# Expert stage of a hybrid attention and mixture-of-experts layer: a third tile form with two half experts in plain fp32, and the shared expert's rows kept on chip

## The chip, the cores and the metric

One NeuronCore of a Trainium2 chip runs the whole layer as one program. The metric is the device time of an execution in microseconds (us); before the change it is 1123.37 us, the median of three runs.

## The reference

The layer is a hybrid attention block, a layer norm, a mixture of experts and a second layer norm, on 512 tokens of width 1024, in fp32. Only the mixture of experts matters here. Each token picks 8 of 64 experts; an expert is two matrices 1024x256 (w1, w3) and one 256x1024 (w2), 3 MB of weights in all, and a shared expert of the same shape sees every token:

```
scores = sigmoid(hf @ w_router)                 # 512 x 64, then top 4 of 8 groups, top 8 experts
hb = silu(x_e @ w1_e[e]) * (x_e @ w3_e[e])      # x_e: the tokens of expert e
acc[t] += (hb @ w2_e[e]) * w[:, None]           # w = weight of the token for e, scaled by 2.5
shared = (silu(hf @ ws1) * (hf @ ws3)) @ ws2
out = layer_norm(ALPHA * h + acc + shared, ln2_g, ln2_b)
```

The routing of the given inputs, counted from the reference, sends 37 to 105 tokens to an expert (mean 64).

## The kernel before

The first 400 us (projections, two attentions) are not touched. The expert stage follows. `order()` ranks the 60 dynamic experts by their number of tokens and lays them in a list `q` = 4..63 (experts 0 to 3 are static, and come first). Work goes by **tiles** of 128 token slots: six tiles hold one expert (four static ones and the two fullest), 29 tiles hold a pair, a fuller and an emptier one; in a pair the rows of both go through both experts, with weight 0 where a row belongs to one alone. For each tile the kernel

- builds the list of its rows (`one_hot`, `slot_mm`, `tile_list`) and gathers them from `hD` in DRAM by an indirect DMA on GpSimd's queue, the **gather** (L1193), two tiles ahead;
- transposes them on TensorE (`xpose`, L1205) and splits them in two fp32r parts;
- for each expert runs 8 k-steps of w1 and w3 side by side (128x512) and, after the SiLU (`act_si`) and a transpose (`act_t`), 4 of w2. Weights come as three 1 MB pages (`expert_load`, L836, SyncE's queue). ScalarE casts each half page to fp32r (L196) and VectorE subtracts for the rest (L197): the **split**. Every product is then three fp32r matmuls (`mm3`, L317 to L319), so 36 for an expert;
- copies the result out of PSUM to a tile `y` (`finish`, L1233, ScalarE, two buffers) and adds its rows into `accD` in DRAM by an indirect accumulating DMA, the **scatter** (L1234, GpSimd's queue). `accD` was filled with ALPHA * h before.

The order of the instructions is written by hand: a list `steps` of (expert, part), with each expert's w2 parts set between the next one's w1/w3 parts. Each engine runs its own instructions strictly in that order. A page of the pool (16 pages) is free for the next load when the split has read it. All scatters write the same DRAM tensor, so each waits for the landing of the one before it; GpSimd's queue issues gathers and scatters in turn. The shared expert (`shared`, `shared_out`) is worked off in small pieces between the steps; each of its four row blocks is added to `accD` by a plain accumulating DMA (L1265) in the same chain.

The last tile is not scattered. The end loads `accD` in four blocks `zs` (L1500, after the last scatter has landed), adds the last tile with TensorE through a 0/1 matrix `back` (L1506, L1508), and normalizes.

Of the kernel before, what the change touches and what calls it, by code (L numbers as in the profile page):

```python
# [19 lines left out]
S, D = 512, 1024  # L20
NE = 64
N_STAT = 4
N_SOLO = 2
N_TILE = N_STAT + N_SOLO + (NE - N_STAT - N_SOLO) // 2
# [14 lines left out]
for _k, _w in (("cb", 128), ("dn", 256), ("dp", 256), ("ut", 128), ("inv", 8), ("tok", 8),  # L39
               ("ident", 128), ("iota1", 128), ("lt", 64), ("lte", 64), ("rq", 128), ("stat", 3)):  # L40
    _C[_k] = (_n, _n + _w)
    _n += _w
# [4 lines left out]
def const_pack():  # L47
# [20 lines left out]
    rq[N_STAT:N_STAT + N_SOLO] = np.arange(N_SOLO)  # L68
    npair = (64 - N_STAT - N_SOLO) // 2
    m = np.arange(npair)  # L70
    rq[N_STAT + N_SOLO::2] = N_SOLO + m
    rq[N_STAT + N_SOLO + 1::2] = N_SOLO + 2 * npair - 1 - m
    put("rq", np.where((np.arange(128) // 64)[None, :] == (np.arange(128) // 64)[:, None], np.tile(rq, 2)[None], -7.0))
    put("stat", np.stack([np.where(e >= N_STAT, 1.0, 0.0), np.where(e < N_STAT, 1000.0 + e, 0.0), e * 1.0], 1))
    inv = np.float32(500000.0) ** (-np.arange(0, 16, 2, dtype=np.float32) / np.float32(16))
# [55 lines left out]
def hybrid_layer_kernel(tc, xT, xn, pos, w_idx, w_blk, w_uk, w_uv, w_ab, w_o, w_r, w_s13, w_s2, w_e, ln, b_gate,  # L131
# [696 lines left out]

    def expert_load(q, eid=None, eng=()):

        src = w_e[q:q + 1] if eid is None else w_e[bass.ds(nc.sync.value_load(eid[0:1, bass.ds(q, 1)], min_val=0,
                                                                             max_val=NE - 1), 1)]
        r = []
        for i in range(3):
            t_ = page([2048], name="we")
            (G if i in eng else nc.sync).dma_start(t_, src[:, :, i * 2048:(i + 1) * 2048].rearrange("a p f -> p (a f)"))  # L836
            r.append(t_)
        return r
# [103 lines left out]
    pos1 = cpool.tile([128, 4, N_TILE], F32, name="pos1")  # L942
# [123 lines left out]
    def one_hot(pos_, i):  # L1066
        oh = t2([4, 128], BF16, name="oh")
        V.tensor_tensor(oh, C("iota1").unsqueeze(1).broadcast_to([128, 4, 128]),
                        pos_[:, :, i].unsqueeze(2).broadcast_to([128, 4, 128]), op=OP.is_equal)
        return oh  # L1070
# [15 lines left out]
    def slot_rows(pl):  # L1086
# [6 lines left out]
        return ii  # L1093
# [6 lines left out]
    def tile_list(oh, qs, tw_):  # L1100
        pl = slot_mm(oh, qs, tw_)
        return [slot_rows(pl), slot_weights(pl, len(qs))]

    tiles = [[q] for q in range(N_STAT + N_SOLO)]
    tiles += [[q, q + 1] for q in range(N_STAT + N_SOLO, NE, 2)]
# [7 lines left out]
    selt = cpool.tile([128, 4, N_TILE], BF16, name="selt")  # L1113

    def order():
# [47 lines left out]
        q0 = N_STAT + N_SOLO  # L1163
        V.tensor_copy(selt[:, :, :q0], selq[:, :, :q0])
        V.tensor_tensor(selt[:, :, q0:], selq[:, :, q0::2], selq[:, :, q0 + 1::2], op=OP.max)
        yield
        places(pos1, selt, N_TILE)
# [4 lines left out]
    def spill():  # L1172
        q0 = N_STAT + N_SOLO
        pc = ps_o()
        for c in range(4):
            mm(pc[0:1, 0:N_TILE], lhsT=ones_b[:, 0:1], rhs=selt[:, c], start=(c == 0), stop=(c == 3))
        nt = t2([3, N_TILE], name="nt")[0:1]
        for b in range(3):
            V.tensor_scalar(nt[:, b], pc[0:1, 0:N_TILE], 128.5 + 128.0 * b, None, op0=OP.is_gt)
        V.tensor_tensor(nt[:, 0], nt[:, 0], nt[:, 1], op=OP.add)  # L1180
        V.tensor_tensor(nt[:, 0], nt[:, 0], nt[:, 2], op=OP.add)
        V.tensor_copy(nbi[:, 0:q0], nt[:, 0, 0:q0])
        V.tensor_copy(nbi[:, q0:NE:2], nt[:, 0, q0:])
        V.tensor_copy(nbi[:, q0 + 1:NE:2], nt[:, 0, q0:])
        nm_ = t2([1], name="nmx")[0:1]
        V.tensor_reduce(nm_, nt[:, 0], axis=AX.X, op=OP.max)
        V.tensor_copy(nbi[:, NE:NE + 1], nm_)
# [10 lines left out]
    def gather(i):  # L1198
        xgs[i] = gather_rows(lists[i][0], xg2[i // 2 % (GA - 1)][:, i % 2])

    def xpose_to(xt, xg, q):
# [4 lines left out]
        split_to(xt[:, 0, 4 * q:4 * q + 4], xt[:, 1, 4 * q:4 * q + 4], pt.rearrange("p (k t) -> p k t", k=4))  # L1206

    def xpose(i, q):
        if q == 0:
            xts[i] = page_x([2, 8, 128], F32R, name="xt")  # L1210
        xpose_to(xts[i], xgs[i], q)
# [7 lines left out]
    def act_t(si):  # L1219
        pt = ps_o()  # L1220
        for f in range(2):
            T.transpose(pt[:, f * 128:(f + 1) * 128], si[:, f * 128:(f + 1) * 128], ident)
        at = t2([2, 2, 128], F32R, name="at")
        split_to(at[:, 0], at[:, 1], pt[:, :256].rearrange("p (f t) -> p f t", f=2))
        return at

    def finish(ii, py, last=False):
        y = t4([D], name="y")
        for n in range(2):
            if n and last:  # L1230
                V.tensor_copy(y[:, n * 512:(n + 1) * 512], py[n])
            else:
                A.copy(y[:, n * 512:(n + 1) * 512], py[n])  # L1233
        G.indirect_dma_start(out=accD[:, :], out_offset=bass.IndirectOffsetOnAxis(ap=ii[:, 0:1], axis=0),  # L1234
                             in_=y, in_offset=None, compute_op=OP.add, bounds_check=S - 1, oob_is_err=False)


    sh_si = {}
# [12 lines left out]
    def shared_out(c):  # L1251
# [6 lines left out]
        y = t4([D], name="ys")  # L1258
# [6 lines left out]
        G.dma_start(accD[c * 128:(c + 1) * 128], y, accum_op=OP.add)  # L1265
# [23 lines left out]
    def prefetch(q):  # L1289
        if q < NE and q not in wts:  # L1290
            wts[q] = expert_load(q, None if q < N_STAT else eid)

    WL = ((),(0,),(),(1,),(2,))
    tile_of = {q: i for i, tl in enumerate(tiles) for q in tl}
    steps = []
    TE = 0
    for q in range(NE + 1):
        if q == NE - 1 and TE:
            steps += [(q - 1, 4), (q - 1, 5)] + [(q, p_) for p_ in range(4)]
            continue  # L1300
        for p_ in range(4):
            if q < NE:
                steps.append((q, p_))
            if q > 0 and p_ in (2, 3):
                steps.append((q - 1, 2 + p_))
    pieces, lpend = {}, []
    todo = iter(steps)

    def split_next(eng=None):
        st_ = next(todo, None)  # L1310
        if st_ is None:
            return
        q, p_ = st_
        if p_ == 0 and eng is None:
            for j in range(q + AHEAD + 1):
                prefetch(j)
# [65 lines left out]
    for q in range(AHEAD):  # L1382
        prefetch(q)
# [3 lines left out]
    with tc.manual_schedule():  # L1387
        for n, (q, p_) in enumerate(steps):
            i = tile_of[q]
            first, last = q == tiles[i][0], q == tiles[i][-1]  # L1390
# [4 lines left out]
            if lpend and p_ == 3:  # L1395
                j, oh = lpend.pop()
                lists[j] = tile_list(oh, tiles[j], tw)
# [7 lines left out]
            if first and p_ == 1 + OHP and N_STAT <= j < len(tiles):  # L1405
                lpend.append((j, one_hot(pos1, j)))
# [6 lines left out]
            if p_ == 4 and q == NE - 2 and TE:  # L1413
                sis[q] = act_si(phs.pop(q), lists[i][1][:, q - tiles[i][0]:][:, 0:1])
                ats[q] = act_t(sis.pop(q))
            if p_ == 0 and q > 0 and q - 1 in phs:
                sis[q - 1] = act_si(phs.pop(q - 1), lists[tile_of[q - 1]][1][:, q - 1 - tiles[tile_of[q - 1]][0]:][:, 0:1])
            while len(pieces) <= LOOK and len(pieces) < len(steps) - n:
                split_next()
            hi, lo = pieces.pop((q, p_))  # L1420
            if p_ < 4:
                if p_ == 0:
                    phs[q] = ps_s()
                for r in range(2):
                    k = 2 * p_ + r
                    mm3(phs[q], xts[i][:, 0, k], xts[i][:, 1, k], hi[:, r], lo[:, r], k == 0, k == 7)
            else:
# [3 lines left out]
                for n_ in range(2):  # L1431
                    mm3(pys[i][n_], ats[q][:, 0, f], ats[q][:, 1, f], hi[:, n_], lo[:, n_], first and f == 0,
                        last and f == 1)
                if last and f == 1 and i < len(tiles) - 1:
                    finish(lists[i][0], pys.pop(i))
            if p_ == 1 and q - 1 in sis:
                ats[q - 1] = act_t(sis.pop(q - 1))
            if p_ == 1 and last and i + 1 < len(tiles):
                xpose(i + 1, 0)
            if p_ == 4 and q + 2 < NE and q + 1 == tiles[tile_of[q + 1]][-1]:  # L1440
                xpose(tile_of[q + 1] + 1, 1)
            if q == 0 and p_ == 2:
                xpose(1, 1)
            if q == NE - 1 and p_ == 3:
                sis[q] = act_si(phs.pop(q), lists[i][1][:, q - tiles[i][0]:][:, 0:1])
                ats[q] = act_t(sis.pop(q))
# [9 lines left out]
    def overflow():  # L1456

        q0 = N_STAT + N_SOLO
        with tc.If(nc.values_load(nbi[0:1, NE:NE + 1], min_val=0, max_val=3) > 0):
            posq = t2([4, NE], name="posq")  # L1460
            V.tensor_copy(posq[:, :, :q0], pos1[:, :, :q0])
            V.tensor_copy(posq[:, :, q0::2], pos1[:, :, q0:])
            V.tensor_copy(posq[:, :, q0 + 1::2], pos1[:, :, q0:])
            with tc.For_i(0, NE, 1) as q:
                with tc.If(nc.values_load(nbi[0:1, bass.ds(q, 1)], min_val=0, max_val=3) > 0):
# [4 lines left out]
                    for b in range(1, 4):  # L1470
# [113 lines left out]
```

## Time and profile before

| | us |
|---|---|
| median of three runs (1122.66 to 1123.41) | 1123.37 |
| profiled execution, its own time | 1120.32 |
| span of its instructions | 1118.5 |
| TensorE (PE) busy | 1080.3 (97%) |
| VectorE (DVE) busy | 899.9 (80%) |
| ScalarE (ACT) busy | 703.4 (63%) |

The profile is of one execution. Busy PE time is modelled, since matmuls overlap each other: a matmul's row shows its latency, and the distance between starts is what it costs. Times in rows are us from the start of the span. A row of a wait names the engine that waited, and what ended the wait as the profile infers it; where that was long done, it was another. For a DMA, "to landing" runs from its issue to the arrival of its semaphore.

### The profile page before, as it was taken

What the parts mean: (1) busy time and instruction counts of PE and PEld (TensorE: products, weight loads), DVE (VectorE), ACT (ScalarE), POOL (GpSimd) and SP (SyncE); (2) the same over time, 40 slices, a digit from 0 to 9 for tenths busy, and PEclk for the clock granted to TensorE, in tenths of its full rate; (3) what the DMA queues carried; (4) which work ended last, traced back from release to release, by engine and by line L of the source; (5) the groups of instructions that cost most, each with busy time, mean ns of one, the idle gap of its engine ahead of it and who ended that gap; (6) DMA issues with size and microseconds to landing.
All of it is one profiled execution on the core that took longest, in us unless ns stands there. A gap on an engine that the chain in (4) does not pass through costs nothing. (4 is left out here: it accounts for less than half of the span.)

```text
span 1118.5 us, 15941 instructions
## 1 busy us (share of the span) xinstructions
PE 1080.3 (97%) x5485; PEld 857.1 (77%) x5486; DVE 899.9 (80%) x1750; ACT 703.4 (63%) x1102; POOL 110.9 (10%) x83
## 2 busy tenths in 40 slices
PE   8999998999999999898999999999999999999995
PEld 7788987877778887476777777788878787878872
DVE  5678998665335978698878878899999999999986
ACT  6554353544542514287767767788888888888873
POOL 0000000000000000122211101221111111212010
PEclk9999999999999999999999999999999999999998
DMA  9414010203016558589999999999999999999943
GB/s 347 138 38 147 5 38 1 76 1 124 28 58 225 209 191 305 187 293 347 344 386 326 359 399 381 374 384 383 402 383 396 384 393 385 387 395 386 373 113 119
DMA packets 50292, 285.49 MB, mean 255 GB/s; under 512 B 7826, under 2 KB 8082, under 8 KB 21920
## 3 DMA queue, kind: packets, MB, share of 16 engines
q1 hardware_dynamic: 37104, 243.21, 55.4%
q0 software_dynamic: 10512, 33.62, 11.9%
q10 hardware_dynamic: 2592, 7.60, 1.9%
q8 instruction: 44, 0.72, 0.3%
q14 instruction: 40, 0.33, 0.1%
HBM read 262.84 MB, written 26.23 MB: 258 GB/s over the span
## 5 line engine op out<-in xcount | busy, mean ns | idle before, releaser
L197 DVE TENSOR_TENSOR sp<-we,sp 128x1024 fp32r<-128x1024 f32 x384 | 452.7, 1218 | 24.6 <-ACT sp L196 22.0
L196 ACT CAST sp<-we 128x1024 fp32r<-128x1024 f32 x384 | 381.8, 1051 | 2.3 <-PE pj L319 2.3
L317 PE MATMUL ps_s<-sp,xt 128*128 128x512 f32 x512 | 216.4, 423 | 0.0
L318 PE MATMUL ps_s<-sp,xt 128*128 128x512 f32 x512 | 202.9, 396 | 0.2
L319 PE MATMUL ps_s<-sp,xt 128*128 128x512 f32 x512 | 201.4, 393 | 0.0
L318 PEld LDWEIGHTS ps_s<-sp,xt 128*128 128x128 f32 x512 | 96.5, 188 | 28.4 <-DVE sp L197 8.9
L317 PEld LDWEIGHTS ps_s<-sp,xt 128*128 128x128 f32 x512 | 96.3, 188 | 20.4 <-issue 2.1
L319 PEld LDWEIGHTS ps_s<-sp,xt 128*128 128x128 f32 x512 | 96.1, 188 | 20.1
L317 PE MATMUL pj<-sp,at 128*128 128x512 f32 x256 | 107.2, 419 | 0.0
L319 PE MATMUL pj<-sp,at 128*128 128x512 f32 x256 | 100.3, 392 | 0.0
L318 PE MATMUL pj<-sp,at 128*128 128x512 f32 x256 | 99.8, 390 | 0.0
L317 PE MATMUL pj<-sp,xh 128*128 128x512 f32 (+1 forms) x224 | 94.6, 425 | 5.0 <-ACT sp L290 5.0
L1234 POOL DMA_INDIRECT accD<-y,ii x34 | 57.3, 1686 | 374.1 <-ACT si L1215 331.1
L318 PE MATMUL pj<-sp,xh 128*128 128x512 f32 (+1 forms) x224 | 87.2, 390 | 0.1
L319 PE MATMUL pj<-sp,xl 128*128 128x512 f32 (+1 forms) x224 | 86.8, 388 | 0.0
L307 DVE TENSOR_TENSOR sp<-raw,sp 128x1024 fp32r<-128x1024 f32 (+2 forms) x45 | 52.2, 1161 | 39.1 <-ACT sp L290 39.1
L290 ACT CAST sp<-raw 128x1024 fp32r<-128x1024 f32 (+2 forms) x45 | 45.1, 1003 | 51.8 <-PE pj L319 49.4
L196 ACT CAST xt<-ps_t 128x512 fp32r<-128x512 f32 x70 | 41.1, 588 | 48.1 <-PE ps_t L1205 46.1
L1233 ACT COPY y<-pj 128x512 f32<-128x512 f32 x68 | 39.9, 588 | 45.3 <-PE pj L319 38.5
L317 PEld LDWEIGHTS pj<-sp,xh 128*128 128x128 f32 x224 | 54.7, 245 | 12.8 <-ACT sp L290 4.7
L615 ACT ACTIVATE aw<-aw,nm 128x256 f32<-128x256 f32 (+3 forms) x64 | 33.5, 526 | 45.0 <-DVE nm L613 45.0
L1193 POOL DMA_INDIRECT xg<-hD,ii x35 | 46.9, 1339 | 128.4 <-PE ps_t L1205 109.5
(390 smaller groups left out, 1813.2 us busy)
## 6 DMA issues: line engine op xcount, KB each, us to landing
we<-in_w_e_dram SPq DMA_DIRECT2D x192, 1024.0 KB, 14.0
raw<-in_w_blk_dram SPq DMA_DIRECT2D x20, 1024.0 KB, 6.2
raw<-in_w_o_dram SPq DMA_DIRECT2D x4, 1024.0 KB, 6.4
rab<-in_w_ab_dram SPq DMA_DIRECT2D x4, 768.0 KB, 4.8
s<-in_w_s_dram SPq DMA_DIRECT2D x3, 1024.0 KB, 6.8
xr<-in_xT_dram SPq DMA_DIRECT2D x8, 256.0 KB, 5.8
hD<-h ACTq DMA_DIRECT2D x4, 512.0 KB, 4.6
accD<-ya ACTq DMA_DIRECT2D x4, 512.0 KB, 4.3
```

Source lines behind the costliest of these rows:

```text
L196: A.copy(hi, raw)
L197: (eng or V).tensor_tensor(lo, raw, hi, op=OP.subtract)
L290: A.copy(hi, part)
L307: V.tensor_tensor(lo, raw, hi, op=OP.subtract)
L317: mm(o_, lhsT=ah, rhs=bh, start=start, stop=False)
L318: mm(o_, lhsT=ah, rhs=bl, start=False, stop=False)
L319: mm(o_, lhsT=al, rhs=bh, start=False, stop=stop)
L615: A.activation(aw[:, hh, :n], aw[:, hh, :n], AF.Exp, scale=0.125, bias=nms[hh], accum_out=den[hh])
L1193: G.indirect_dma_start(out=xg, out_offset=None, in_=hD[:, :], in_offset=bass.IndirectOffsetOnAxis(ap=ii[:, 0:1], axis=0), bounds_check=S - ...
L1233: A.copy(y[:, n * 512:(n + 1) * 512], py[n])
L1234: G.indirect_dma_start(out=accD[:, :], out_offset=bass.IndirectOffsetOnAxis(ap=ii[:, 0:1], axis=0), in_=y, in_offset=None, compute_op=OP.a ...
```

## The change

- The list of dynamic experts is laid out anew. 16 pairs of the middle ranks stay as pairs (q = 4..35). Then follow seven groups of four experts (q = 36..63): two of the 14 fullest, each alone in a tile, and a **half tile** with two of the 14 emptiest, one in slots 0 to 63, the other in slots 64 to 127. There are 41 tiles instead of 35.
- In a half tile nothing is split. The rows are transposed to plain fp32 (`xtn`), and each product is one plain fp32 matmul per expert, with 64 stationary columns and 64 output partitions: `mm(phs[u][hs], ...)`. The weight pages are read by TensorE itself, and are free only when it has done so. The six loads of two experts are issued in turns.
- A half tile is scattered by two DMAs, `ii` for the first 64 slots and `jj` for the others (slots below 64 get an index out of bounds and are skipped), since a row may be in both halves.
- The shared expert's rows are no longer added to `accD`. They stay in the pages of `hT` until the end (two pages fewer for weights), and VectorE adds them to `zs` there: four adds of 128x1024.
- The branch for overfull tiles is adapted: a half overflows above 64 tokens. Counted from the reference, the fullest of the 14 emptiest has 53 and the fullest pair of the middle 121 rows, so it is not taken.

```diff
+plan = [([q], q, False) for q in range(N_STAT)]
+plan += [([Q_BOTH + 2 * m, Q_BOTH + 2 * m + 1], Q_BOTH + m, False) for m in range(N_BOTH)]
+for m in range(N_HALF):
+    q, c = Q_TURN + 4 * m, C_TURN + 4 * m
+    plan += [([q], c, False), ([q + 1], c + 1, False), ([q + 2, q + 3], c + 2, True)]
...
-    def finish(ii, py, last=False):
+    def finish(ii, py, half=False):
         y = t4([D], name="y")
...
+        for rows, n in zip(ii, (64, 128) if half else (128,)):
+            G.indirect_dma_start(out=accD[:, :], out_offset=bass.IndirectOffsetOnAxis(ap=rows[:n, 0:1], axis=0),
+                                 in_=y[:n], in_offset=None, compute_op=OP.add, bounds_check=S - 1, oob_is_err=False)
...
-        y = t4([D], name="ys")
+        y = ysh[c] = hT[c // 2][:, c % 2].rearrange("p k t -> p (k t)")
...
-        G.dma_start(accD[c * 128:(c + 1) * 128], y, accum_op=OP.add)
...
                 for r in range(2):
                     k = 2 * p_ + r
+                    if half:
+                        for q, hs in zip(qs, HALF):
+                            w13 = wts[q][k // 4].rearrange("p (k n) -> p k n", k=4)
+                            mm(phs[u][hs], lhsT=xts[i][:, k, hs], rhs=w13[:, k % 4], start=(k == 0), stop=(k == 7))
+                    else:
+                        mm3(phs[u], xts[i][:, 0, k], xts[i][:, 1, k], hi[:, r], lo[:, r], k == 0, k == 7)
...
         for c in range(4):
             nc.sync.dma_start(zs[c], accD[c * 128:(c + 1) * 128])
+            V.tensor_tensor(zs[c], zs[c], ysh[c], op=OP.add)
```

GpSimd's queue in the last third of the expert stage, before (a name in brackets is a semaphore waited for, the DMASW ones those of its own DMAs):

```order
L1193 DMA xg_4124<-hD,ii 128x1024 [waits DMASW3_49,DVE_49,PE_49]
L1234 DMA accD<-y,ii 512x1024 [waits DMASW6_49,Activation_49]
L1193 DMA xg_4124<-hD,ii 128x1024 [waits DMASW5_49,DVE_49,PE_49]
L1234 DMA accD<-y,ii 512x1024 [waits DMASW0_49,Activation_49]
L1193 DMA xg_4124<-hD,ii 128x1024 [waits DMASW7_49,DVE_49,PE_49]
L1234 DMA accD<-y,ii 512x1024 [waits DMASW2_49,Activation_49]
```

One gather and one scatter stand there for every two experts. The same queue and place, in the changed kernel, for one group of four experts:

```order
L1272 DMA accD<-y,ii 512x1024 [waits DMASW3_49,Activation_49]
L1272 DMA accD<-y,jj 512x1024 [waits DMASW5_49]
L1222 DMA xg_4124<-hD,ii 128x1024 [waits DMASW2_49,DVE_49,PE_49]
L1272 DMA accD<-y,ii 512x1024 [waits DMASW6_49,Activation_49]
L1222 DMA xg_4124<-hD,ii 128x1024 [waits DMASW4_49,DVE_49,PE_49]
L1272 DMA accD<-y,ii 512x1024 [waits DMASW0_49,Activation_49]
L1222 DMA xg_4124<-hD,ii 128x1024 [waits DMASW7_49,DVE_49,PE_49]
L1272 DMA accD<-y,ii 512x1024 [waits DMASW2_49,Activation_49]
L1272 DMA accD<-y,jj 512x1024 [waits DMASW4_49]
```

Four scatters (`ii` and `jj` of a half tile, then two tiles with one expert) and three gathers stand there for four experts; each scatter waits for the semaphore of the scatter before it, and a gather stands behind a scatter that waits.

VectorE at the end, behind the branch for overfull tiles, before (BN_STATS begins the last normalization):

```order
L1459 UNCONDITIONAL_BRANCH
L1532 BN_STATS bs_11434<-pj 128x6 x2
L1533 BN_AGGR mv_11435<-bs_11434 128x2
L1535 TENSOR_SCALAR nm_11432<-mv_11435 128x1
L1536 COPY var_11433<-mv_11435 128x1
```

The statistics come first there. The same place of the changed kernel (`z` are the blocks `zs`, `hT` the pages with the shared rows):

```order
L1525 UNCONDITIONAL_BRANCH
L1570 TENSOR_TENSOR z<-z,hT_3808 128x1024 x2
L1570 TENSOR_TENSOR z<-z,hT_4086 128x1024 x2
L1583 MEMSET eps 128x1
L1602 BN_STATS bs_11162<-pj 128x6 x2
```

The four adds of the shared rows now stand ahead of the first statistics.

## Rows read from the trace of the kernel before

**Rows 1.** Busy time by stretch: stretch, length, engines, PEclk, DMA share, GB/s
```profile
950.00:1000.00 50.00, 50.00 (x248) 40.28 (x247) 47.27 (x62) 41.19 (x56) 9.09 (x6) 1.00 1.02 386
1092.40:1118.50 26.10, 13.99 (x33) 6.00 (x32) 17.02 (x43) 7.92 (x21) 0.00 (x0) 0.83 0.28 110
```

**Rows 2.** Waits of 740 to 1060: who waited for whom, total, times, longest
```profile
POOL accD L1234 <- ACT si L1215: 187.6, 17, 11.1
PEld ps_s L318 <- DVE sp L197: 5.6, 18, 0.3
```

**Rows 3.** Timeline of TensorE: start, duration, engine, line, operation, count
```profile
915.14 0.39 PE L317 MATMUL ps_s<-sp,xt 128*128 128x512 f32 x1
...
917.18 0.39 PE L317 MATMUL ps_s<-sp,xt 128*128 128x512 f32 x1
```

**Rows 4.** Timeline of ScalarE: copies of two pairs' results, q 34,35 first
```profile
841.49 1.27 ACT L1233 COPY y<-pj 128x512 f32<-128x512 f32 x2 [0.96 <-PE pj L319]
...
859.84 1.27 ACT L1233 COPY y<-pj 128x512 f32<-128x512 f32 x2 [0.99 <-PE pj L319]
```

**Rows 5.** Groups of 800 to 1050: the split on VectorE, busy, mean ns, idle
```profile
L197 DVE TENSOR_TENSOR sp<-we,sp 128x1024 fp32r<-128x1024 f32 x165 | 194.2, 1218 | 8.7 <-ACT sp L196 6.9 <-DMA we<-in_w_e_dram 1.4
```

**Rows 6.** DMA of 950 to 1000 by queue; weight loads, issue to landing
```profile
q1 hardware_dynamic: 2317, 16.88, 82.4%
q0 software_dynamic: 720, 2.39, 19.1%
...
we<-in_w_e_dram SPq DMA_DIRECT2D x17, 1024.0 KB, 22.5
```

**Rows 7.** Weight loads of the whole span: durations, first and last issue
```profile
L836 SPq DMA_DIRECT2D we<-in_w_e_dram x192: 327/333/517, 386.3 to 1044.5; - x192
```

**Rows 8.** Timeline of TensorE: plain fp32 records at full and at half width
```profile
437.45 3.65 PE L1244 MATMUL pj<-s,hT 128*128 128x512 f32 x8
```

**Rows 9.** Timeline of TensorE: products with 64 stationary columns, halves in turn
```profile
269.01 1.09 PE L694 MATMUL ps_o<-aw,av 128*64 128x128 f32 x16
```

**Rows 10.** Timeline of GpSimd's queue, 494 to 554, tiles with one expert
```profile
496.20 1.79 POOL L1234 DMA_INDIRECT accD<-y,ii  x1 [5.75 <-ACT si L1215]
...
507.56 2.17 POOL L1234 DMA_INDIRECT accD<-y,ii  x1 [8.22 <-ACT sp L196]
...
518.63 1.60 POOL L1234 DMA_INDIRECT accD<-y,ii  x1 [7.56 <-ACT si L1215]
...
542.75 1.58 POOL L1234 DMA_INDIRECT accD<-y,ii  x1 [9.01 <-ACT si L1215]
...
564.12 2.51 POOL L1234 DMA_INDIRECT accD<-y,ii  x1 [8.28 <-ACT sp L196]
```

**Rows 11.** Timeline of ScalarE in that stretch: copies of results out of PSUM
```profile
504.53 1.26 ACT L1233 COPY y<-pj 128x512 f32<-128x512 f32 x2
...
541.08 1.08 ACT L1233 COPY y<-pj 128x512 f32<-128x512 f32 x2 [3.71 <-DMA accD<-y,ii]
```

**Rows 12.** Scatters issued from 564 to 736, then from 752 to 1045: issue to landing
```profile
DMA to landing us min/median/max: 8.4/10.4/11.4
...
DMA to landing us min/median/max: 10.1/10.5/11.2
```

**Rows 13.** DMA issues of 500 to 550: scatters and gathers, count, median us to landing
```profile
accD<-y,ii POOLq DMA_INDIRECT x4, 10.2
xg<-hD,ii POOLq DMA_INDIRECT x3, 12.1
```

**Rows 14.** Timeline of the end: last scatter, loads of accD, first sums
```profile
1080.48 1.55 POOL L1234 DMA_INDIRECT accD<-y,ii  x1 [16.66 <-ACT si L1215]
...
1086.64 2.51 SPq L1500 DMA_DIRECT2D z<-accD  x4
...
1092.87 1.96 PE L1506 MATMUL pj<-z,c_all 128*128 128x512 f32 x4 [0.45 <-ACTq L1459]
```

More of the change, by code (lines that the diff above doesn't have):

```diff
@@ L1084, in hybrid_layer_kernel, with slot_rows @@
     rowf, last_rows = [], []
-    def slot_rows(pl):
+    def slot_rows(pl, half=False):
         lo_ = small([1], "li", bufs=4)
@@ L1092, in slot_rows @@
         rowf[:] = [(pl, lo_)]
-        return ii
+        if not half:
+            return [ii]
+        jj = small([1], "jj", I32, bufs=6)
+        V.scalar_tensor_tensor(jj, lo_, C("half"), pl[:, 0:1], op0=OP.add, op1=OP.add)
+        return [ii, jj]
     def slot_weights(pl, n):
@@ L1098, in slot_weights, with half_weights, tile_list @@
         return wv
-    def tile_list(oh, qs, tw_):
-        pl = slot_mm(oh, qs, tw_)
-        return [slot_rows(pl), slot_weights(pl, len(qs))]
-    tiles = [[q] for q in range(N_STAT + N_SOLO)]
-    tiles += [[q, q + 1] for q in range(N_STAT + N_SOLO, NE, 2)]
+    def half_weights(pl):
+        wv = small([2], "wv", bufs=8)
+        for m, hs in enumerate(HALF):
+            V.tensor_reduce(wv[hs, 0:1], pl[hs, 2 + 3 * m:5 + 3 * m], axis=AX.X, op=OP.add)
+        return wv
+    def tile_list(oh, qs, tw_, half=False):
+        pl = slot_mm(oh, qs, tw_)
+        return [slot_rows(pl, half), half_weights(pl) if half else slot_weights(pl, len(qs))]
+    plan = [([q], q, False) for q in range(N_STAT)]
[3 more added lines that the diff above has]
+        plan += [([q], c, False), ([q + 1], c + 1, False), ([q + 2, q + 3], c + 2, True)]
+    tiles = [t[0] for t in plan]
     lists = {}
@@ L1112, in hybrid_layer_kernel @@
     selq = cpool.tile([128, 4, NE], BF16, name="selq")
-    selt = cpool.tile([128, 4, N_TILE], BF16, name="selt")
+    selt = cpool.tile([128, 4, N_COL], BF16, name="selt")
     def order():
@@ L1217, in act_si, with act_t @@
         return si
-    def act_t(si):
+    def act_t(si, parts=True):
         pt = ps_o()
@@ L1379, in hybrid_layer_kernel @@
         fill_sh(FL[4])
-    for q in range(AHEAD):
-        prefetch(q)
+    prefetch(AHEAD - 1)
     LG = (1,)
@@ L1387, in hybrid_layer_kernel, with weights_of @@
     with tc.manual_schedule():
-        for n, (q, p_) in enumerate(steps):
-            i = tile_of[q]
-            first, last = q == tiles[i][0], q == tiles[i][-1]
+        def weights_of(u):
+            qs, i, _ = units[u]
+            w_ = lists[i][1][:, qs[0] - tiles[i][0]:]
+            return w_[:, 0:1]
+        for n, (u, p_) in enumerate(steps):
+            qs, i, half = units[u]
+            first, last = first_of[u], last_of[u]
             if n in OST:
@@ L1396, in hybrid_layer_kernel @@
                 j, oh = lpend.pop()
-                lists[j] = tile_list(oh, tiles[j], tw)
+                lists[j] = tile_list(oh, tiles[j], tw, plan[j][2])
                 if j == len(tiles) - 1:
@@ L1469, in overflow @@
                     V.tensor_copy(wc, tw[:, :, bass.ds(q, 1)])
-                    for b in range(1, 4):
+                    for b in range(1, 5):
                         pb = t2([4, 1], name="pb")
```

225 lines of the change are left out of this document (130 added, 95 removed).

## The prediction

> **What bounds the kernel now.** I read the busy time by stretch first, then the waits of the expert stage, then the DMA queues, then GpSimd's queue. In the expert stage TensorE has no idle time, VectorE is at 47 of 50 us, and the DMA engines are fully busy too [rows 1]. The waits decide between them: from 740 to 1060 TensorE waits 5.6 us in all, and the long wait of the stretch is GpSimd's queue, for work to scatter [rows 2]. So TensorE sets the pace. Nine fp32r matmuls start within 2.04 us, 0.227 each [rows 3]: 36 of them are 8.2 us for an expert, and a pair comes every 18.35 us [rows 4], so 16.3 us of matmuls and 2.0 of transposes and lists. Four experts take 36.7 us. The DMA is close behind: of 50 us the weight queue has 41.2 for 16.1 pages of 1.05 MB, 2.56 us a page, and the queue of gathers and scatters 9.6 us for 2.7 tiles, 3.5 us a tile [rows 6]. Four experts ask 12 x 2.56 + 2 x 3.5 = 37.7 us; as the shares sum to 102%, take 37. The last page is issued at 1044.5 [rows 7], and with the 17 to 19 us that loads take then it lands near 1063, while the end's first sums start at 1092.87 [rows 14], right behind the last expert's matmuls: the weights are some 20 us ahead of their use. That is all that a faster TensorE could win before the DMA stops it.
>
> **The change, part by part.**
>
> *TensorE, half tiles.* A plain fp32 product at full width is two records, 8 of which take 3.65 us, some 0.44 each [rows 8]. With 64 stationary columns and the two output halves in turn, 16 records of 128 columns take 1.09 us [rows 9], 0.055 to 0.068 each (with and without the drain of the last one), half of a quarter of 0.44: the halves overlap. A half tile has 12 products x 2 halves x 2 records of 512 columns, 48 x 0.22 = 10.5 us (up to 13.1; 21 if they did not overlap). A group of four costs 16.3 + 10.5 + three tiles of overhead at 1.5 to 2.0 = 32 us instead of 36.7. VectorE and ScalarE lose 12 of 24 splits, 14.6 us of VectorE [rows 5], beside other work.
>
> *DMA.* Weights stay. Rows move with little change (in a group 252 to 283 instead of 236, as pairs no longer share rows), so 38 us a group instead of 37. DMA alone would then set the pace at 38.
>
> *The chain of scatters.* Each scatter waits for the one before it to land; nothing may overlap. Before, one scatter per pair lands after 10.4 or 10.5 us, out of 18.35 [rows 12]: 7 us to spare. What happens when tiles come faster is seen at the start of the stage, where tiles hold one expert. The result of the tile scattered at 507.56 was in `y` at 505.8 [rows 11], but the scatter before it, of 496.20 [rows 10], landed about 506.4 by that stretch's median of 10.2 [rows 13]. The same again at 518.63: 11.1 to 11.4 us from scatter to scatter, so 0.8 us or a little more between a landing and the next issue. At 541.08 ScalarE itself stood 3.7 us for a `y` buffer that a scatter still held [rows 11], and behind it the casts, and so TensorE. The gather behind a scatter takes 12.1 us to land [rows 13].
> After the change a group has four scatters. Three are of 128 slots: landing 8.4 to 11.4 us, median 10.4 [rows 12], plus 0.8. The number of rows in them hardly matters, as those at 496 to 531 with 59 to 105 rows take as long as those with 118. I take 9.8 + 0.8 = 10.6, below the median since the weight queue will have some slack. The scatter of 64 slots has no row of its own; 6.1 us is the last one of the program, with the DMA all but empty (1080.48 to the loads that wait for it, 1086.64 [rows 14]), and 11.2 the highest; I take 7.5 + 0.8 = 8.3, as half the slots halve the data's part but not the lead. A group: 3 x 10.6 + 8.3 = 40 us (37 to 45). This is over the DMA's 38 and TensorE's 32, and 3.4 over the 36.7 of before. The chain becomes the bound.
>
> *By the Trainium skill* a scatter is much shorter: "DMA: Bandwidth & Descriptors", section "Anatomy of one DMA", fits a GpSimd-issued DMA as 2.0 us plus bytes over 436 GB/s, an estimate of about 2.8 us for 85 rows of 4 KB and 2.5 for a half. The trace disagrees with 10.4 us beside loaded weight queues [rows 12]. By that page the chain would be some 14 us a group and would never show; what follows from this is rival one.
>
> *Start of the chain.* Before, the pair q = 34,35 is copied out from 841.5 to 842.8 [rows 4] and scattered right behind, at 843. The change makes the two tiles with the fullest experts a pair: 24.1 us for two such tiles (518.63 to 542.75) become 21.4 (542.75 to 564.12) [rows 10], -3 us; that the shared rows' four DMAs leave the chain is worth nothing more here, as pairs leave 7 us of it idle. So this scatter goes out at 840, and lands 10.5 + 0.8 later: the chain of the seven groups starts at 851.5, and its `y` is ready by then. The first scatter of group seven goes out 6 x 40 later, less 4 for the last `jj`, which finds the weights loaded: 1087.5. Its landing (6.1 + 0.8) lets the last one go at 1094.4, landed at 1100.5.
>
> *The end.* The loads of `accD` wait for that landing, before as after. Before, from 1086.64 to the first sums at 1092.87 are 6.2 us [rows 14]. After: 1106.7, plus one add of 128x1024, 1.2 us by the nearest row [rows 5], 1107.9. From the first sums to the end were 25.6 us; the other three adds stand ahead of the statistics on VectorE, about +1 us as the loads arrive in that time, and TensorE, idle since its last matmul about 10 us earlier, starts at the lower clock (0.83 granted in that stretch already before [rows 1]), +2 us. The end is at 1107.9 + 25.6 + 3 = 1136.5 against 1118.5: **+18 us**. Gathers behind waiting scatters, loads that hold two pages fewer, and VectorE's small list work cost nothing beyond this while the chain is late. The profiled execution took 1120.3 us, so 1138.3; the median of runs was 3.05 us above it: **1141 us**.
>
> **Rivals.**
> *One, the chain does not bind,* because scatters land much sooner once the splits are fewer and the weights' queue thinner. Then DMA sets the pace at 38: last page near 1068, last scatter out near 1061 and landed at 1071, `accD` loaded and added at 1079, end at 1105: -13 us, 1110. For it: the one landing of 6.1 us. Against it: in the stretch of 564 to 736, when the weights were not pressed either, the lowest is 8.4 [rows 12]. It decides when a group's four scatters take under 37 us, 9.3 each with the wait.
> *Two, no difference.* At 37 us a group the chain's lateness and the end's add just cancel the 3 us won early. 1121 to 1126.
> *Three, the halves do not overlap at 512 columns.* TensorE then takes 16.3 + 21 + 5 = 42 us a group, 5.6 over before, seven times: +39 less 3, plus 3 at the end, 1162. Against it speak the 16 records [rows 9].
> The slower side is thus held by one mechanism, the chain, with its place (GpSimd's queue), its price (3.4 us a group and 11 us at the end) and its threshold (37 us).
>
> **How the numbers follow.** Chain binds: 0.70, 1141, with its bounds 1127 to 1167. Halves don't overlap: 0.04, 1162. No difference: 0.07. Chain doesn't bind: 0.19, 1100 to 1120. The range that leaves out 2 in 10 goes from 1110, into rival one, to 1165. Under 0.2%, 2.2 us, a measurement of this kernel can't tell from no change. Faster 0.19, same 0.07, slower 0.74.
>
> **What would show it.** In the changed profile, from about 850 on: scatters on GpSimd's queue 0.8 us after each other's landing, four in 40 us; copies to `y` on ScalarE that wait for DMA; TensorE idle a fifth of the stretch, at its transposes and behind the splits; 48 half-width records of a half tile in about 10.5 us; the DMA share below 1. The loads of `accD` at the end come well after TensorE's last expert matmul. It is wrong if scatters of a half tile land in 5 us or the others in 8, if the chain shows idle time between landing and next issue, or if the seven groups pass in under 37 us each.

## The result and the profile after

The changed kernel takes 1164.43 us (median of four runs, 1163.39 to 1166.64) against 1123.39 before on the same chip: ratio 1.0369, 95% interval 1.0351 to 1.0387, so some 41 us slower. The profiled execution has a span of 1162.9 us against 1118.5. The direction was forecast, the amount (+18) was not. Ratios, here and below, leave out the one execution at a much lower granted clock (of e6: 1492.9 us, clock 0.654).

Busy time of two stretches in the groups of four experts (columns as in [rows 1]):

```profile
950.00:1000.00 50.00, 40.23 (x197) 23.80 (x196) 24.47 (x42) 21.82 (x33) 10.99 (x7) 0.86 0.82 295
1000.00:1050.00 50.00, 39.54 (x200) 24.80 (x199) 25.13 (x40) 24.73 (x38) 12.34 (x9) 0.90 0.89 329
```

Beside [rows 1], VectorE is down from 47 to 24 us and TensorE from 50 to 40, which now stands idle a fifth of the time and shows granted clocks of 0.86 and 0.90, a mix of the 1.2 and 2.4 GHz levels, where it had 1.00. The DMA share is below 1 as well. No engine is full any more, so waits set the pace. The waits of 860 to 1100 tell whose:

```profile
POOL accD L1272 <- ACT si L1249: 94.3, 10, 11.0
...
PE ps_t L1234 <- DMA xg<-hD,ii: 50.6, 10, 9.2
POOL accD L1272 <- DMA accD<-y,jj: 31.2, 4, 8.0
POOL accD L1272 <- DMA accD<-y,ii: 30.6, 4, 8.0
```

GpSimd's queue waits for scatters to land, as forecast (the third and fourth row; of the ten waits in the first row, which names ScalarE, four are for landings too, since they end 0.7 us after one, and six end with the copy of the second full expert's result). The second row is the new one, which the prediction does not have: TensorE waits 50.6 us for gathers. One group, as the chain of work that ended last shows it (start, duration, what):

```profile
930.72 10.38 DMA accD<-y,jj
...
942.24 6.99 DMA accD<-y,ii
949.26 5.54 issue
955.03 11.29 DMA accD<-y,ii
966.36 0.47 issue
967.05 2.12 POOL accD L1272
969.18 7.10 issue
976.50 10.30 DMA accD<-y,jj
986.84 0.69 issue
987.76 7.15 DMA accD<-y,ii
```

From one first full expert's scatter (942.24) to the next (987.76) it is 45.5 us. In it are four landings (6.99, 11.29, about 9.0 for `ii` of 967.05, and 10.30: 37.6 in all), three turnarounds of 0.5 to 1 us, and 5.8 us from 949.2 to 955.0 in which **no scatter is under way**. GpSimd's queue, TensorE and ScalarE around that hole:

```profile
930.72 2.18 POOL L1272 DMA_INDIRECT accD<-y,jj  x1 [7.52 <-DMA accD<-y,ii]
933.20 1.07 POOL L1222 DMA_INDIRECT xg<-hD,ii  x1 [0.30 <-issue]
942.24 1.56 POOL L1272 DMA_INDIRECT accD<-y,ii  x1 [7.96 <-issue]
...
955.03 1.58 POOL L1272 DMA_INDIRECT accD<-y,ii  x1 [9.86 <-ACT si L1249]
```

```profile
944.38 1.09 PE L1234 MATMUL ps_t<-c_all,xg 128*128 128x128 f32 x4 [8.74 <-DMA xg<-hD,ii]
...
953.29 1.28 ACT L1270 COPY y<-pj 128x512 f32<-128x512 f32 x2 [1.41 <-PE pj L326]
...
964.79 0.59 ACT L1270 COPY y<-pj 128x512 f32<-128x512 f32 x1 [0.30 <-PE pj L1496]
```

The gather of 933.20 stood in the queue behind the scatter `jj`, which itself had to wait for `ii` to land. TensorE waited 8.74 us for the gathered rows, at 944.38. Its transposes stand, in TensorE's order, ahead of the last matmuls of the second full expert, so that expert's result was copied out only at 953.29 to 954.57 and scattered at 955.03. That scatter delays the next `ii`, and `ii` delays the next `jj`. This is a closed ring: `jj` issued 930.72, gather 2.5 us later, 11.2 to its rows, 10.6 of TensorE and copy, 12.0 for the scatter of the second full expert, 9.5 for `ii`, and `jj` again at 976.50: 45.8 us. There is a second way round that is nearly as long: the same gather also delays the half tile's own result, which was copied out only at 965.38 (the last row), 0.9 us before the landing that `ii` waited for. So cutting the chain alone can win little here; e5 below tries that.

The end, where the last landing is waited for:

```profile
1123.42 1.56 POOL L1272 DMA_INDIRECT accD<-y,ii  x1 [5.37 <-DMA accD<-y,ii]
...
1130.30 2.04 SPq L1569 DMA_DIRECT2D z<-accD  x4
...
1133.60 2.36 DVE L1570 TENSOR_TENSOR z<-z,hT 128x1024 f32<-128x1024 f32 x2 [1.53 <-DMA z<-accD]
1134.97 2.79 PE L1576 MATMUL pj<-z,c_all 128*128 128x512 f32 x3 [3.67 <-DVE z L1570]
```

### The profile page after: what moved, and what is told of

It is laid out like the page before. It is cut to its first block, busy times and chain, and to the rows that moved or that the text cites. A ratio compares the mean times of both kernels' runs of the same rounds, so it can differ in the third digit from the quotient of the medians.

```text
span 1162.9 us, 15599 instructions
## 1 busy us (share of the span) xinstructions
PE 1067.3 (92%) x5399; PEld 797.3 (69%) x5400; DVE 812.5 (70%) x1685; ACT 630.6 (54%) x1026; POOL 130.9 (11%) x97
## 3 DMA queue, kind: packets, MB, share of 16 engines
q0 software_dynamic: 12144, 32.18, 11.1%
## 4 chain that ended last, share of the span: by engine, by line
PE 60%; DMA 16%; DVE 11%; issue 7%; ACT 3%; POOL 1%; POOLq 0%; SPq 0%; ACTq 0%; DVEq 0%
PE pj L324 10%; PE pj L326 9%; PE pj L325 9%; DMA accD<-y,ii 9%; PE ps_s L324 6%; PE ps_s L325 6%; PE ps_s L326 6%; DMA accD<-y,jj 4%; PE pj L1282 2%; DMA xg<-hD,ii 2%; DVE sp L204 2%; PE ps_t L1234 1%; DMA we<-in_w_e_dram 1%; PE pj L1300 1%; DVE score L509 1%
## 5 line engine op out<-in xcount | busy, mean ns | idle before, releaser
L204 DVE TENSOR_TENSOR sp<-we,sp 128x1024 fp32r<-128x1024 f32 x300 | 355.3, 1220 | 42.9 <-ACT sp L203 42.5
L203 ACT CAST sp<-we 128x1024 fp32r<-128x1024 f32 x300 | 300.5, 1052 | 2.3 <-PE pj L326 2.3
L324 PE MATMUL ps_s<-sp,xt 128*128 128x512 f32 x400 | 171.8, 430 | 0.0
L325 PE MATMUL ps_s<-sp,xt 128*128 128x512 f32 x400 | 158.5, 396 | 0.2 <-DVE sp L204 0.2
L326 PE MATMUL ps_s<-sp,xt 128*128 128x512 f32 x400 | 157.3, 393 | 0.0
L1272 POOL DMA_INDIRECT accD<-y,ii x40 | 65.3, 1632 | 405.8 <-ACT si L1249 303.5
L204 DVE TENSOR_TENSOR xt<-ps_t,xt 128x512 fp32r<-128x512 f32 x68 | 46.7, 686 | 84.3 <-ACT xt L203 84.1
L1234 PE MATMUL ps_t<-c_all,xg 128*128 128x128 f32 x328 | 52.4, 284 | 53.7 <-DMA xg<-hD,ii 53.4
L324 PEld LDWEIGHTS ps_s<-sp,xt 128*128 128x128 f32 x400 | 75.3, 188 | 21.6 <-ACT y L1270 4.9
L325 PEld LDWEIGHTS ps_s<-sp,xt 128*128 128x128 f32 x400 | 75.7, 189 | 20.3 <-DVE sp L204 4.4
L324 PE MATMUL pj<-sp,at 128*128 128x512 f32 x200 | 87.7, 439 | 0.5 <-ACT at L203 0.5
L326 PEld LDWEIGHTS ps_s<-sp,xt 128*128 128x128 f32 x400 | 75.4, 188 | 16.2
L1234 PEld LDWEIGHTS ps_t<-c_all,xg 128*128 128x128 f32 x328 | 39.8, 145 | 66.5 <-issue 46.6
L326 PE MATMUL pj<-sp,at 128*128 128x512 f32 x200 | 79.3, 397 | 0.0
L325 PE MATMUL pj<-sp,at 128*128 128x512 f32 x200 | 79.1, 396 | 0.0
L1270 ACT COPY y<-pj 128x512 f32<-128x512 f32 x80 | 46.9, 587 | 52.4 <-PE pj L326 41.0
L297 ACT CAST sp<-raw 128x1024 fp32r<-128x1024 f32 (+2 forms) x45 | 45.1, 1003 | 53.4 <-PE pj L326 50.1
```

The source lines that it names most:

```text
L203: A.copy(hi, raw)
L204: (eng or V).tensor_tensor(lo, raw, hi, op=OP.subtract)
L297: A.copy(hi, part)
L324: mm(o_, lhsT=ah, rhs=bh, start=start, stop=False)
L325: mm(o_, lhsT=ah, rhs=bl, start=False, stop=False)
L326: mm(o_, lhsT=al, rhs=bh, start=False, stop=stop)
```

## The experiments

Ratios are to runs of the kernel before on the same chip as the experiment. The experiments used two chips, which gave it 1120.6 to 1121.9 us, so times below stand some 2 us lower than beside 1123.4, and the ratios are what is compared.

| | us | ratio (95% interval) |
|---|---|---|
| changed kernel | 1164.4 | 1.0369 (1.0351 to 1.0387) |
| e1 gathers ahead of scatters | 1146.9 | 1.0237 (1.0221 to 1.0252) |
| e2 without second scatter of halves | 1133.0 | 1.0107 (1.0091 to 1.0122) |
| e3 before, shared rows kept | 1125.5 | 1.0048 (1.0034 to 1.0062) |
| e5 two sums | 1157.6 | 1.0322 (1.0304 to 1.0339) |
| e6 two sums, gathers ahead | 1128.2 | 1.0063 (1.0042 to 1.0084) |
| e7 the same, three groups | 1117.6 | 0.9971 (0.9960 to 0.9982) |
| e8 list of 64 places | 1153.9 | 1.0306 (1.0283 to 1.0329) |
| e9 third tile split | 1143.4 | 1.0176 (1.0155 to 1.0197) |
| e10 e7 with list of 64 | 1119.3 | 0.9978 (0.9967 to 0.9990) |
| e11 e10 with third buffer | 1125.0 | 1.0030 (1.0016 to 1.0044) |

**e1. The queue's order alone.** Theory: the gather behind `jj` closes the ring. Rival: the hole is TensorE's own work.

```diff
-            if p_ == 0 and first and n and i + GA < len(tiles):
+            if p_ == 0 and first and n and i + GA < len(tiles) and i <= C_TURN:
                 gather(i + GA)
...
+                if last and f == 1 and C_TURN <= i + 1 and i + 4 < len(tiles):
+                    gather(i + 4)
                 if last and f == 1 and i < len(tiles) - 1:
                     finish(lists[i][0], pys.pop(i), half)
```

> The changed kernel with one edit: in the groups of four, a gather is put on GpSimd's queue ahead of the scatter behind which it stood (its list and its buffer are free by then); nothing else differs. Measured in the changed kernel: seven groups at 45.3 us, of which the four landings are 36.7, the turnarounds 3.2 and about 5.4 a stretch in which no scatter is under way, between the landing of the first full expert's scatter and the issue of the second's. Theory: that stretch exists because the gather of the next tile waits behind the second scatter of the half tile, so that TensorE gets its rows late and the second full expert's result with them. Then a group falls to 40 to 43 us and the time from 1164 to 1134 to 1150. Rival: the idle stretch is TensorE's own work, or the landings only fill it by growing as more transfers overlap; then the group stays at 45 and the time within 3 us of 1164.

Its queue in one group:

```profile
959.27 2.10 POOL L1272 DMA_INDIRECT accD<-y,ii  x1 [7.83 <-ACT y L1270]
968.04 1.56 POOL L1272 DMA_INDIRECT accD<-y,jj  x1 [6.67 <-DMA accD<-y,ii]
969.90 1.82 POOL L1222 DMA_INDIRECT xg<-hD,ii  x1 [0.30 <-PE ps_s L1486]
978.89 1.57 POOL L1272 DMA_INDIRECT accD<-y,ii  x1 [7.17 <-ACT y L1270]
...
989.82 1.57 POOL L1272 DMA_INDIRECT accD<-y,ii  x1 [7.21 <-DMA accD<-y,ii]
...
1000.94 1.73 POOL L1272 DMA_INDIRECT accD<-y,ii  x1 [8.19 <-ACT y L1270]
```

The hole is gone: four scatters follow each other at 8.8, 10.9, 10.9 and 11.1 us, 41.7 for the group, and four groups from 876.44 to 1044.35 take 42.0 each. TensorE's waits for gathers of 900 to 1080 fall to 2.7 us. This is the chain that was forecast, bare; it holds the result buffers, and ScalarE now waits for them:

```profile
ACT y L1270 <- DMA accD<-y,jj: 27.0, 3, 11.8
```

**e5 and e6. The chain alone, and both.** A second sum `accE` in DRAM takes the half tiles, so the chains don't wait for each other; the shared rows are written there first, and so don't hold two pages until the end.

```diff
+    accE = dpool.tile([S, D], F32, name="accE")
...
-            G.indirect_dma_start(out=accD[:, :], out_offset=...
+            G.indirect_dma_start(out=(accE if half else accD)[:, :], out_offset=...
...
+        nc.scalar.dma_start(accE[c * 128:(c + 1) * 128], y)
...
-            V.tensor_tensor(zs[c], zs[c], ysh[c], op=OP.add)
+            V.tensor_tensor(zs[c], zs[c], ze[c], op=OP.add)
```

> The changed kernel with a second sum in DRAM: the half tiles are scattered into it, the others into the old one, so the two chains don't wait for each other. The second sum is filled with the shared expert's rows by plain DMAs in the early part of the stage, so these don't stay on chip; the end loads both sums and VectorE adds them. GpSimd's queue keeps its order, gathers stand behind waiting scatters. Theory (the loop through the queue): the chain is no longer the bound (23 and 20 us a group), yet the gather still stands behind the second scatter of the half tile: from there 13.5 to the rows, 10.7 to the second full expert's result, about 10 to the half tile's, 9.5 to its second scatter, 43 to 45 a group: 1148 to 1164 us, most of the loss remains. Rival (the chain alone is the cause, the queue's order nothing): a group falls to the DMA's 39, 1125 to 1135.

> The same two sums, and the gathers of the groups ahead of the scatters in the queue. Nothing of chain or queue is left then. Theory: the weights' DMA is the bound, as it was with the second scatter left out (five groups in 194.5 us, 38.9 each): the same 38 to 39.5 a group, 1124 to 1136 us, so still not faster than the kernel before, whose TensorE needs 36.7. Rival (DMA keeps up and the plain products show what they save on TensorE, 32 us a group): below 1112.

With the chain cut in two and the queue left, the first full experts' scatters come every 44.1 us (892.71 to 1069.28 in four groups), hardly less than 45, and TensorE still waits for gathers, 44.8 us of 900 to 1080 in e5:

```profile
PE ps_t L1235 <- DMA xg<-hD,ii: 44.8, 9, 9.1
```

With both edits (e6) TensorE's waits for gathers are gone, and the weights are what is waited for; the DMA is full. `jj` still waits in GpSimd's queue for `ii` to land (first row), with a gather and a scatter behind it, so e6 is not quite free of chain and queue:

```profile
POOL accE L1273 <- DMA accE<-y,ii: 38.3, 4, 11.6
ACT sp L203 <- DMA we<-in_w_e_dram: 34.2, 4, 10.4
```

```profile
1000.00:1050.00 50.00, 41.09 (x198) 24.95 (x200) 25.87 (x45) 23.47 (x35) 10.31 (x7) 0.87 1.01 372
```

As loss over before: neither edit 3.7%, queue alone 2.4%, chain alone 3.2%, both 0.6%. The two edits together give more than the sum of each alone, as two limits of nearly the same length (42 and 44 us a group) lie over each other. Six groups of e6 take 36.5 us in the mean, but 32.4, 35.3 and 35.4 at first, while the lead of the weights lasts, and 38.1, 41.2 and 37.0 after it.

**e2. One scatter fewer.** (The rows of the second halves are left out of the sum.)

```diff
-        for rows, n in zip(ii, (64, 128) if half else (128,)):
+        for rows, n in zip(ii, (64,) if half else (128,)):
```

> The changed kernel without the second scatter of every half tile: the rows of the second halves (their 64 slots) are left out of the sum, all else stands. Theory (a loop through the queue): without it the gather stands behind the first scatter of the half tile, and the loop of gather 13.5, TensorE 10.7, scatter of the second full expert 12 is 36 us, the three remaining landings 32, the DMA 38: a group of 38 to 39, so 6 x 7 = 42 us less, and some 6 at the end where the last chain is shorter by one: 1112 to 1125. Rival (TensorE's lower clock or the plain fp32 products set the group's time, the chain only fits itself to it): the group stays above 43, the time above 1148.

1133.0, so the direction is the theory's, but the time lies above its range. The first full experts' scatters show why: 853.07, 889.52, 923.89, 958.34, 1002.50, 1037.60, 1083.85. Three groups pass in 34 to 36 us, then one takes 44 and one 46, in which the casts wait for weights:

```profile
ACT sp L203 <- DMA we<-in_w_e_dram: 32.8, 4, 13.6
```

The mean is 38.5, as the theory had it (38 to 39) and near the DMA's 38 of the prediction: seven groups at that pace lose what the plain products save. The rival, a group above 43 whatever the chain does, is out.

**e8. What makes a landing long.** The second scatter gets a list of 64 places (four small matmuls make it), in place of 128 with half out of bounds.

```diff
-        for rows, n in zip(ii, (64, 128) if half else (128,)):
+        for rows, hs in zip(ii, HALF if half else (slice(0, 128),)):
-            ... ap=rows[:n, 0:1] ... in_=y[:n] ...
+            ... ap=rows[:hs.stop - hs.start, 0:1] ... in_=y[hs] ...
```

> The changed kernel, in which the second scatter of a half tile has a list of 64 places of its own and takes the lower 64 rows of the result, where it had a list of 128 of which half was out of bounds; four small matmuls more for each half tile. In the changed kernel the first scatter (64 places) lands after 8.2 to 9.0 us, the second (128, half of them skipped) after 10.3 to 10.8. Theory: the places in the list, not the rows that are moved, make up this part; the second lands after 8 to 9 too, the loop is 1.5 to 2.5 a group shorter, 1149 to 1156 us. Rival (the second is longer since it follows the first, or since its rows are the same number as before): 10 to 11 us again, 1161 to 1168.

DMA issues of 900 to 1070 of the changed kernel, then of e8 (count, median us to landing):

```profile
accD<-y,jj POOLq DMA_INDIRECT x4, 10.3
```

```profile
accD<-y,jj POOLq DMA_INDIRECT x4, 8.0
```

The same 37 to 50 rows (counted from the reference) are added, in 2.3 us less: the places in the list count. The group falls by 1.8 us, from 45.3 to 43.5, and the loss from 3.7% to 3.1%. A shorter step of the ring shortens the group nearly by as much.

**e3. The shared rows alone**, put into the kernel before.

```diff
-        y = t4([D], name="ys")
+        y = ysh[c] = hT[c // 2][:, c % 2].rearrange("p k t -> p (k t)")
...
-        G.dma_start(accD[c * 128:(c + 1) * 128], y, accum_op=OP.add)
...
             nc.sync.dma_start(zs[c], accD[c * 128:(c + 1) * 128])
+            V.tensor_tensor(zs[c], zs[c], ysh[c], op=OP.add)
```

> The kernel before with the second part of the change alone: the shared expert's rows stay in the pages that held the transposed tokens, their four accumulating DMAs are gone, and VectorE adds them to the loaded rows at the end; two pages fewer take weights. Theory: it costs one add ahead of the sums and three ahead of the first statistics, 1 to 4 us, and nothing in the stage as TensorE sets the pace there: 1124 to 1128. Rival: the four DMAs out of the chain give the early tiles something back, or fewer pages let weights come late: under 1122, or over 1130.

The ratio 1.0048 is 5.4 us on 1120.6 (3.8 to 6.9), at or above the upper end of the 1 to 4 that the theory put on it. In its profile the last scatter goes out 1.4 us later than in [rows 14], and the first sums 3.8 us later, behind the adds:

```profile
1095.31 4.63 DVE L1500 TENSOR_TENSOR z<-z,hT 128x1024 f32<-128x1024 f32 x4 [0.76 <-DVEq L1458]
1096.68 3.38 PE L1506 MATMUL pj<-z,c_all 128*128 128x512 f32 x4 [2.86 <-DVE z L1500]
```

**e9 (and e4). The tiles without plain fp32.** The third tile of a group becomes an ordinary split pair with one scatter.

```diff
-        plan += [([q], c, False), ([q + 1], c + 1, False), ([q + 2, q + 3], c + 2, True)]
+        plan += [([q], c, False), ([q + 1], c + 1, False), ([q + 2, q + 3], c + 2, False)]
...
+        V.tensor_tensor(selt[:, :, C_TURN + 2::4], selq[:, :, Q_TURN + 2::4], selq[:, :, Q_TURN + 3::4], op=OP.max)
...
-            V.tensor_scalar(nt[:, C_TURN + a::4], pc[0:1, C_TURN + a:N_COL:4], 64.5, None, op0=OP.is_gt)
+            V.tensor_scalar(nt[:, C_TURN + a::4], pc[0:1, C_TURN + a:N_COL:4], 128.5, None, op0=OP.is_gt)
```

The first try left the last line at 64.5; the branch for overfull tiles was taken, the time was 2028 us, and nothing can be read from it. What was expected of both:

> The changed kernel with the plan of its tiles and the shared rows kept as they are, but the third tile of a group is an ordinary pair, split in fp32r: its rows go through both experts with weight 0 where they don't belong, one scatter for the tile. Theory: three scatters need 33 us a group, so the chain has slack; TensorE sets the pace again with four experts of 36 fp32r matmuls (32.7) and three tiles of overhead (2.0 each) = 38.7 to 39.5 us a group, 2 to 3 over before: 1130 to 1145. Rival: gathers behind scatters hold TensorE also here, or three tiles for four experts are bad whatever the arithmetic: over 1150.

> The changed kernel with the plan of its tiles and the shared rows kept on chip as they are, but the third tile of a group is an ordinary pair, split in fp32r, with one scatter; the bound above which a tile counts as overfull is 128 rows for it, as for every pair (in the run with the name of the same edit it was left at 64, so the branch for overfull tiles was taken seven times). Theory: three scatters need 33 us a group, so the chain has slack; TensorE sets the pace with four experts of 36 matmuls (32.7) and three tiles of overhead (1.5 to 2.0 each), 37.5 to 39.5 us a group, 1 to 3 over before, and the adds at the end cost 3.5: 1130 to 1145. Rival: gathers behind scatters hold TensorE here too, a group over 42, over 1155.

Second try, 900 to 950:

```profile
900.00:950.00 50.00, 49.96 (x261) 40.28 (x260) 48.44 (x63) 41.72 (x59) 12.44 (x8) 1.00 1.01 371
```

TensorE is full again, at clock 1.00, and a group takes 38.1 us (880.38 to 1032.97 in four): 1.4 over before for one more tile. Three tiles for four experts are thus not what costs 45 us; still, this plan is slower than before, by 1.8%. Its last three scatters leave at 1075.50, 1086.56 and 1097.97, the last two 2.0 and 4.7 us after their results were copied out (1084.58 and 1093.24): the chain bites at its end here too.

**e7, e10 and e11. A version that uses the lead only.** Both edits of e6, and N_HALF = 3 in place of 7.

> The same with three groups of four at the end of the stage in place of seven, so 24 pairs, and the six fullest and the six emptiest experts in the groups. Theory: the weights are 20 us ahead of TensorE when the groups begin, so for three groups TensorE can use up that lead: 32 to 34 us a group instead of 36.7, 8 to 14 us won, 3.5 to 5 given back for the adds at the end: 1112 to 1120 against 1121 to 1123 before. Rival (the lead is not there for it, as the loads go on only when pages come free): 1120 to 1130.

0.9971: 0.3% faster than the kernel before, and so than the changed one. The lead of the weights is there, and TensorE doesn't wait for them:

```profile
1000.00:1050.00 50.00, 50.00 (x266) 30.64 (x262) 32.74 (x54) 29.98 (x45) 16.40 (x10) 1.00 1.02 389
```

From 1001.42 to 1064.85 two groups pass in 31.7 us each, 5.0 less than before. Three such groups would be 15 us; 3.5 are left. The adds at the end take back some 5, if they cost what they do in e3; the rest was not taken apart, but the last scatters are late in the records, and the last copy waited for a buffer:

```profile
1070.70 1.07 ACT L1271 COPY y<-pj 128x512 f32<-128x512 f32 x2 [6.48 <-DMA accE<-y,jj]
1074.88 1.54 POOL L1273 DMA_INDIRECT accD<-y,ii  x1 [8.48 <-DMA accD<-y,ii]
```

e10 adds the list of 64 of e8 to this; e11 adds a third result buffer to e10 and takes one page from the pool.

> Three groups with two sums and gathers first, and the list of 64 places for the second scatter of a half tile. There, near the end, the copy of the last full expert's result stood 6.5 us for a result buffer that such a second scatter still held. Theory: it lands 2 us sooner, the copy and the last scatter go out 2 us sooner, and the end comes 1 to 2.5 us sooner: 1114.5 to 1117 beside 1117.6. Rival (the last scatter waits for the one before it on its own chain as well): within 1 us of 1117.6.

> The same with three result buffers in place of two, paid for with one page of the pool (15 in place of 16, one fewer for weights). Theory: the copy no longer waits for a buffer, and the last scatter goes out when the one before it has landed: 2 to 4 us sooner than with two: 1111 to 1115. Rival: a page fewer takes from the lead of the weights that the three groups live on, and gives it all back: 1117 to 1125.

Neither gains: 0.9978 is the same as 0.9971 within their intervals, 1.0030 is a loss. The same two places in e10:

```profile
1071.07 1.07 ACT L1276 COPY y<-pj 128x512 f32<-128x512 f32 x2 [6.28 <-DMA accE<-y,jj]
...
1076.64 1.56 POOL L1278 DMA_INDIRECT accD<-y,ii  x1 [9.98 <-DMA accD<-y,ii]
```

The copy still waits: `jj`, issued at 1063.25, frees the buffer after 7.8 us with 64 places, in e7 after 7.7 us with 128 (issued at 1062.99). Here, beside a scatter of the other chain, the shorter list won nothing, and the theory's first step failed. The rival holds as well: the last scatter leaves 4.5 us after the copy has ended, behind the landing on its own chain. In e11 the copy waits for no buffer, but the last scatter for its own chain all the same. In its profiled execution (span 1129.7, one of its longer ones) it goes out at 1086.55, 11.7 us later than in e7. Of these, 8.7 are there before the groups begin: the same pair's scatter leaves at 868.28, in e7 at 859.63. If the page that is missing is the cause, it acts early in the stage and not on the lead of the groups; this was not tried apart.

## Why the prediction was wrong

By its steps:

- **TensorE, half tiles: right.** The halves overlap. 32 records of the last half tile take 7.09 us, 0.222 each, and its 16 of w2 3.65, 0.228: 10.7 us in all, where 10.5 was forecast. Rival three is out.

```profile
1118.64 7.09 PE L1486 MATMUL ps_s<-we,xtn 128*64 128x512 f32 x32
...
1127.65 3.65 PE L1496 MATMUL pj<-we,atn 128*64 128x512 f32 x16 [0.46 <-ACT atn L1260]
```

- **The chain's landings: right in sum, by luck.** Forecast 3 x 9.8 + 7.5 = 36.9 a group, measured 37.6 in the group above. Three were longer (`ii` 9.0 for 7.5, `jj` 10.3 and the second full expert's 11.3 for 9.8), and the first full expert's, 7.0 for 9.8, made up for them. It flies while TensorE waits, and from 945 to 950 the DMA share is down to 0.67; that it is short for this reason was not tried. It is not on the ring either: in the first two groups it took 10.8 and 10.2, the hole behind it was only 1.9 and 3.1 us, and the rounds were nearly as long (44.2 and 45.1).
- **The step that failed** is the sentence that gathers behind waiting scatters "cost nothing beyond this while the chain is late". The sum took the chain as a line, in which each result is ready when its turn comes. It is a ring: the late `jj` holds back a gather, the gather TensorE, and TensorE the result that the chain needs next. It is 45.8 us a round, against 40 in the sum. The scatter of the first full expert of group seven went out at 1116.5 where 1087.5 was forecast, 29 us late, of which the start of the chain is 1.5. e1 shows the step by itself: with the gathers ahead, a group is 42.0 us, within the 37 to 45 that were given for the chain alone. That 1164 lies inside the 1127 to 1167 given for "chain binds" is luck: the upper end stood for long landings (11.4), and the landings were not long.
- **The end: 2.8 us too long.** From the last landing (some 1129.7) to the end are 33.2 us where 6.2 + 1.2 + 25.6 + 3 = 36 were summed: the first load of `accD` landed after 3.2 us, where in the kernel before it took 6.3 (the first number of each row below, the kernel before above the changed one; why they differ is open). The last landing is 29.2 late, and +29.2 - 2.8 = 26.4 is the difference of the spans, 1162.9 to 1136.5.

```profile
DMA to landing us min/median/max: 6.3/6.7/7.1
...
DMA to landing us min/median/max: 3.2/5.3/7.0
```

- **The start of the chain: right.** The first scatter of group one goes out at 852.99, forecast 851.5.
- **Rival one's price was wrong too.** e6 comes nearest to its case, as TensorE no longer waits for a gather. It comes out 0.6% slower, not 13 us faster. Its DMA pace was near (38 a group), but the last weight page is issued at 1053.5 where before it was 1044.5, and the last scatter lands at 1092, not 1071. The last page lands at 1078 (1053.5 and 24.6 us), 10 later than put there, and the last two scatters stand 9.3 us apart on their chain; further it was not taken apart. As e6 and e7 read, a faster TensorE wins the lead of the weights, once: in e6 the groups get longer after the third, and seven don't win more than three.
- **Two readings behind that rival don't hold.** The last loads of the kernel before took not 17 to 19 us but 22.3 to 23.4 (those issued from 1038 on, below), so the last page landed at 1068 instead of 1063, and the lead of the weights is 5 us shorter than stated. And the stretch of 564 to 736, named as one in which the weights were not pressed, has a DMA share of 0.99 to 1.02, so its landings say nothing of a thinner queue. Neither is a term of the sum.

```profile
DMA to landing us min/median/max: 22.3/23.2/23.4
```

- What would show it: the forecast named "if the chain shows idle time between landing and next issue" as a sign against it. That is the sign seen. Another sign that it named for its own case, copies to `y` on ScalarE that wait for DMA, is missing: from 840 to 1120 no such wait is on record in the changed kernel, while e1, with the queue's order mended, has them (27.0 us). The results were late, not held up.

So the chain was the right place and a real limit of 42 us, and the queue a second limit of 44 to 45 that lay over it. Of the 3.7%, both together make up 3.1. The 0.6 that is left is near the 0.5 that the adds cost in e3; and nothing of TensorE's saving is seen over the whole stage, since a group of e6 takes 36.5 us in the mean, beside 36.7 before.

## What to carry to other kernels

When a queue issues both the results of one tile and the inputs of another, follow it round: ask which later result needs the input that stands behind a waiting output, and add up the whole ring, not one engine's or one chain's share. A chain of landings that "binds" can be shorter than a ring through it, so an idle stretch between a landing and the next issue is to be looked for. Where two streams are nearly balanced, as TensorE and the weights' DMA here, ask how far one is ahead of the other: a faster engine won that lead and no more, so spend the change on as many tiles as the lead pays for.

## What the runs showed of the hardware

A scatter's time went by the places in its list rather than by the rows that it moved: 10.3 us for 128 places of which half were skipped, 8.0 for 64 places with the same rows, beside weight loads. In the kernel before, lists of 128 with 59 to 105 valid rows took 10.2 us in the median [rows 13] and those with some 118 took 10.4 and 10.5 [rows 12]. With few weights under way the same forms are shorter: in e8, where the last `ii` goes out at 1094.95 and `jj` at 1099.85, the 64 places land in under 4.9 us, and the last three lists of 128 of the changed kernel took 6.1 to 6.9. It is not so everywhere: in e10, beside a scatter of the other chain, 64 places took as long as 128 in e7.

```profile
1094.95 1.43 POOL L1277 DMA_INDIRECT accD<-y,ii  x1 [8.29 <-DMA accD<-y,ii]
1099.85 1.44 POOL L1277 DMA_INDIRECT accD<-y,jj  x1 [3.46 <-DMA accD<-y,ii]
```
